# A hybrid decoder trunk: scan states from products of rounded parts, key tiles split a step later, two units multiplied and then added

## The chip, the cores and the metric

The kernel runs on one core of one Trainium2 chip. The metric is the device time of one execution in microseconds (us). The kernel before takes 2855.78 us, the median of three executions (2853.89 to 2859.62).

The names of the engines are those of the profile: PE multiplies matrices (PEld loads its weights), DVE does elementwise work, ACT evaluates functions and copies, POOL does elementwise work too, SP issues DMAs. Each takes its instructions in the order in which the program lists them; between engines they wait for each other.

## The reference, cut to what matters

One sequence of 1024 tokens with 16 learned meta tokens ahead (L = 1040), width 1024, two layers. Layer 0 is a state space mixer (32 heads of 64, in 4 groups that share B and C, state size 128) and a convolutional feed-forward network; layer 1 is a stick-breaking attention (16 heads of 64) and another such network. All inputs and outputs are float32. The part of the mixer that the change touches:

```python
xdt = x_c * dt_c[..., None]
cb = jnp.einsum('bclgn,bcsgn->bgcls', c_c, b_c)
y_diag = jnp.einsum('bgcls,bgecls,bcsgep->bclgep', cb, decay_in, xdt)
decay_to_end = jnp.exp(a_cs[..., -1:] - a_cs)
chunk_states = jnp.einsum('bclgn,bgecl,bclgep->cbgepn', b_c, decay_to_end, xdt)
...
y_off = jnp.einsum('bclgn,cbgepn,bgecl->bclgep', c_c, prev_states, jnp.exp(a_cs))
y = (y_diag + y_off).reshape(b, nc * Q, SSM_D_INNER)[:, pf:pf + L]
```

`chunk_states` is what one chunk of tokens adds to the state; a scan over the chunks scales the state and adds it. The attention multiplies queries by keys, and its output goes through a projection `o @ sb_w_o` that is added to the residual stream `h`.

## The kernel before

**Arithmetic.** Nearly every product of two float32 matrices is made of three products of rounded parts: each operand is split into a high part (a copy rounded to the type fp32r, on ACT) and a low part (the operand minus the high part, on DVE or POOL), and `mm3` (L206) issues high x high, high x low and low x high into one PSUM bank. A few products take float32 operands directly: those of the scan (`cb`, `S`, `y`), transposes and sums.

**The mixer** (`mixer`, L823) scans 4 groups, each over 9 chunks of 116 tokens (the last has 112). The projections of the layer are not done ahead of the scan but between its parts: `work` is a stream of tiles, each one projection of 128 output channels for a third of the tokens (24 products on PE), and the table SHARES says how many tiles go into each chunk: 2 in most chunks of group 0 and group 3, 3 or 4 in groups 1 and 2. A tile ends in a PSUM bank; there are three banks in turn, so a tile needs the bank of the tile three before it. A tile of a convolved projection (all tiles in group 0) is read from its bank by ACT (L336) and three times by DVE (L339), and a SiLU on ACT follows later (L614); a tile of the gate (all in group 3) is read by a SiLU on ACT (L646), then squared on ACT (L658) and worked into sums and products on DVE (L664, L653).

One chunk runs so, in the order of the program:
- `ssd_front` (L759): PE transposes B and x into PSUM and multiplies C by B (`cb`, `px`); ACT copies the transposed B to `bk` (L778); DVE makes `cbm` (L780), `xdt` (L782) and the decayed product `D` (L783); POOL scales `xdt` to `xde`.
- the tiles of `work`. After the first of them the DMAs for the next chunk's `D` and `E` are issued; after the second, DVE subtracts in `D` (L752, 8 instructions) and ACT takes its exponential (L753), for the next chunk.
- `ssd_back` (L789): PE makes the state product `S` from `bk` and `xde` (L799), and DVE adds it to the state (L805); PE makes `y`, 8 products of `xdt` with `D` (L810) and 8 of the state with `E` (L812); DVE adds `y` to x (L814); POOL scales the state for the next chunk.
- POOL scales `E` for the next chunk with C (four pieces), and the next `ssd_front` begins. So POOL's order is: state, `E`, `xde`, and where a weight tile is split in between, its low part `wl`.

Inside the scan the order of PE, DVE, ACT and POOL is that of the program text (a manual schedule); elsewhere, and for SP's queue, a scheduler sets it.

**The attention** runs 8 pairs of heads with 18 steps each. In a step `weigh` multiplies queries by keys into one double bank (`lg`, L1653), ACT takes two sigmoids of it (L1654, L1655), DVE scans and multiplies (L1664, L1665). The projections of the next pair are made in halves between the steps (`half`, L1559). When a key tile is finished, DVE scales it out of its bank (L1577) and returns a function that splits it: `key` (L1583) copies its high part on ACT (L1588), subtracts on DVE (L1589) and issues three DMAs. That function runs in the next step.

**The end of the attention** interleaves the last turns with units of the output projection (`o_blocks`, L1808): a unit is 12 products and one add to `h` on DVE (`accumulate`, L528; the add is L538). Its last part has its own double bank `both`, one half for each of two units.

Of the kernel before, what the change touches and what calls it, by code (L numbers as in the profile page):

```python
# [8 lines left out]
F32 = mybir.dt.float32  # L9
F32R = mybir.dt.float32r  # L10
# [95 lines left out]
class Trunk:  # L106
    def __init__(self, ctx, tc, a):
        self.tc, self.nc, self.a = tc, tc.nc, a
        nc = self.nc
        self.cp = ctx.enter_context(tc.tile_pool(name="cp", bufs=1))  # L110
        self.qp = ctx.enter_context(tc.tile_pool(name="qp", bufs=NQ))
        self.tmps = ctx.enter_context(tc.tile_pool(name="up", bufs=8))
        self.wp = ctx.enter_context(tc.tile_pool(name="wp", bufs=3))
        self.mp = ctx.enter_context(tc.tile_pool(name="mp", bufs=2, space=bass.MemoryType.PSUM))
        self.sp = ctx.enter_context(tc.tile_pool(name="sp", bufs=SMB, space=bass.MemoryType.PSUM))
        self.dp = ctx.enter_context(tc.tile_pool(name="dp", bufs=1, space=bass.MemoryType.DRAM))
        self.lp = None
        self.n = 0
        self.open = []
        self.hold = self.copy_tie = self.silu_tie = None  # L120
        self.consts()


# [404 lines left out]
    def accumulate(self, h, f, s0, n, w, ks, front=0, bank=None, base=0, new=False):  # L528

        ps = (bank or (self.ex if f % 3 == 2 else self.mm))("acc")  # L530
        c, o = slice(s0 - base, s0 - base + n), slice(front + s0, front + s0 + n)
        for i, (hi, lo) in enumerate(ks):
            wh, wl = w(i, f)
            self.mm3(ps[:, :n], wh, wl, hi[:, c], lo[:, c], i == 0, i == len(ks) - 1)
        if new:
            self.nc.vector.tensor_copy(h[f][:, o], ps[:, :n])
        else:
            self.nc.vector.tensor_tensor(h[f][:, o], h[f][:, o], ps[:, :n], op=ALU.add)  # L538

# [219 lines left out]
    def ssd_front(self, g, x, bt, ct, c, dk, pool):  # L759
# [14 lines left out]
        px = px[:n].rearrange("p (h d) -> p h d", h=GH)  # L774
        bk = xde = None
        if c < 8:
            bk = pool.tile([P, P], F32, tag="bk", name=self.nm("bk"), bufs=2)
            nc.scalar.activation(bk[:n], pcb[:n, P : 2 * P], AF.Copy)  # L778
        cbm = pool.tile([P, CB], F32, tag="cbm", name=self.nm("cbm"), bufs=2)
        tt(cbm[:n, :n], pcb[:n, :n], self.past[:n, :n], op=ALU.mult)  # L780
        xdt = pool.tile([P, GH, 64], F32, tag="xdt", name=self.nm("xdt"), bufs=2)
        tt(xdt[:n], px, self.cols[:n, 0, cc, h0 : h0 + GH].unsqueeze(2).to_broadcast([n, GH, 64]), op=ALU.mult)  # L782
        tt(dk, dk, cbm[:n, :n].unsqueeze(1).to_broadcast([n, GH, n]), op=ALU.mult)  # L783
        if c < 8:
            xde = pool.tile([P, GH, 64], F32, tag="xde", name=self.nm("xde"), bufs=2)
            pieces(nc.gpsimd, xde[:n], xdt[:n], self.cols[:n, 2, cc, h0 : h0 + GH].unsqueeze(2).to_broadcast([n, GH, 64]), ALU.mult)
        return xdt, xde, bk

    def ssd_back(self, g, x, c, dk, ce, xdt, xde, bk, states, pool):  # L789

# [3 lines left out]
        cc = 3 * (c % 3) + c // 3  # L794
        e = t0 + n
        state, new = states
        if c < 8:
            ps = self.lg("S")
            nc.tensor.matmul(ps, bk[:n], xde[:n].rearrange("p h d -> p (h d)"), start=True, stop=True)  # L799
            psv = ps.rearrange("p (h d) -> p h d", h=GH)  # L800
            if c == 0:
                new = pool.tile([P, GH, 64], F32, tag="state", name=self.nm("state"), bufs=2)
                nc.scalar.activation(new, psv, AF.Copy)
            else:
                nc.vector.tensor_tensor(new, new, psv, op=ALU.add)  # L805
        py = self.sm("y")
        for i in range(GH):
            q, r = i // 2, 64 * (i % 2)
            y = py[r : r + 64, q * CB : q * CB + n]
            nc.tensor.matmul(y, xdt[:n, i, :], dk[:, i, :], start=True, stop=c == 0)  # L810
            if c:
                nc.tensor.matmul(y, state[:, i, :], ce[:, i, :], start=False, stop=True)  # L812
        for q in range(4):
            nc.vector.scalar_tensor_tensor(x[q][:, t0:e], x[q][:, t0:e], self.par("d_skip", 4 * g + q),  # L814
                                           py[:, q * CB : q * CB + n], op0=ALU.mult, op1=ALU.add)
# [699 lines left out]
    def heads(self, u, p, pool):  # L1515
# [4 lines left out]
        class Pair:  # L1520
# [38 lines left out]
            def half(me, kind, j, h, bank=None, parts=2):  # L1559
# [15 lines left out]
                t = self.tmp(kind)  # L1575
                if kind == "k":
                    nc.vector.tensor_tensor(t[:, :n], ps[:, :n], u[KD][:, o:e], op=ALU.mult)  # L1577
                    return [lambda: me.key(j, t)]
                nc.scalar.activation(t[:, :n], ps[:, :n], AF.Copy)
                me.late.append((j, t))  # L1580
                return []
# [137 lines left out]
    def attention(self, u, pool, hd):  # L1719
# [34 lines left out]
        for kind, j, bank in (("k", 0, self.mm), ("q", 0, self.mm), ("k", 1, self.sm), ("q", 1, self.ex)):  # L1754
            for h in range(2):
                for f in first.half(kind, j, h, bank):
                    f()
            if (kind, j) == ("k", 0):
                self.late_factors()
        self.token_factors(u[KD], pool)  # L1760
        for p in range(PAIRS):
            prev = None
            for n, (i, jj) in enumerate(steps):
# [14 lines left out]
                for own, pair in now.items():  # L1778
                    if p + 1 < PAIRS and (own, n) in halves:
                        late += pair.half(*halves[own, n])  # L1780
                for f in todo + chores[:1]:
                    f()
                del chores[:1]
                for own, pair in now.items():
# [4 lines left out]
        both = self.lg2("acc")  # L1789
        banks = iter([lambda s, a=a: both[:, a] for a in range(2)])  # L1790
        self.unit_bank = lambda s: next(banks, self.mm)(s)
        while turns or ready:
            next(behind)
            next(behind)
            flush(0)
        return od, behind

# [260 lines left out]
```

## Time and profile before

| | us |
|---|---|
| median of three executions | 2855.78 |
| the profiled execution, its own time | 2855.13 |
| its span, first to last instruction | 2853.3 |
| PE busy | 2809.2 |
| DVE busy | 2065.4 |
| ACT busy | 1580.2 |
| POOL busy | 1578.6 |
| scan of the mixer, about | 119 to 614 |
| attention, about | 1545 to 2080 |

The times of the stages are stretches of the span, read from the first and last rows of the stage's lines. In the rows of a timeline the columns are the start, the duration, the engine, the line, the operation, what is written and read with sizes, how many instructions in a row are merged, and in brackets how long the engine sat idle before it and what ended that. A product of float32 operands shows as two instructions. In rows of groups the columns are the count, then busy us and mean ns.

### The profile page before, as it was taken

To read this page: it belongs to the slowest core of one execution; us is meant where nothing else is said; L and a number is where in the kernel's file an instruction comes from. 1 tells how busy PE (TensorE), PEld (TensorE's weight loads), DVE (VectorE), ACT (ScalarE), POOL (GpSimd) and SP (SyncE) were. 2 spreads that over 40 slices of the span, in tenths; PEclk is the share of its full clock that TensorE was granted. 3 is DMA by queue.
4 is the path that set the end of the run, shared out by engine and by line. 5 is a ranking of instruction groups with operands and counts; after the bars stand their busy time and mean duration, and the time that the engine had idled before them with its cause. 6 is when DMAs were issued, how large, how long until landed. Compare 5 with 4: busy or idle time off the path is not lost.

```text
span 2853.3 us, 56464 instructions
## 1 busy us (share of the span) xinstructions
PE 2809.2 (98%) x21251; PEld 2691.9 (94%) x21251; DVE 2065.4 (72%) x3936; ACT 1580.2 (55%) x3077; POOL 1578.6 (55%) x2144
## 2 busy tenths in 40 slices
PE   8999999999999999999999999999999999999998
PEld 7989999999999999999999999999899999999888
DVE  5676666668487676767886888888749676766776
ACT  5554554543256555555335777777536555555433
POOL 2366455553519888867763212112254888886881
PEclk9999999999999999999999999999999999999999
DMA  4333333343413222235142222222532222225331
GB/s 119 86 112 93 121 83 125 116 136 101 120 64 96 78 80 78 79 135 176 49 142 77 74 73 69 80 70 57 184 131 77 82 80 82 75 82 185 111 104 67
DMA packets 141740, 281.78 MB, mean 99 GB/s; under 512 B 16307, under 2 KB 71740, under 8 KB 141468
## 3 DMA queue, kind: packets, MB, share of 16 engines
q1 hardware_dynamic: 135844, 267.01, 29.8%
q0 software_dynamic: 2048, 6.49, 0.6%
q10 hardware_dynamic: 3576, 4.67, 0.5%
q8 instruction: 168, 2.75, 0.4%
q14 instruction: 104, 0.85, 0.1%
HBM read 207.79 MB, written 55.42 MB: 92 GB/s over the span
## 4 chain that ended last, share of the span: by engine, by line
PE 91%; DVE 4%; ACT 2%; POOL 1%; issue 1%; DMA 0%; SPq 0%; ACTq 0%; DVEq 0%; POOLq 0%
PE p L209 10%; PE p L210 10%; PE p L211 10%; PE acc L209 8%; PE acc L211 8%; PE acc L210 8%; PE pj L209 8%; PE pj L210 8%; PE pj L211 8%; PE po L1710 3%; PE lg L1653 2%; PE wT L1687 2%; PE y L810 1%; PE S L799 1%; PE y L812 1%; PE ms L1069 1%
## 5 line engine op out<-in xcount | busy, mean ns | idle before, releaser
L102 POOL TENSOR_TENSOR wl<-w,wh 128x256 fp32r<-128x256 f32 x760 | 678.9, 923 | 352.2 <-ACT wh L196 225.4
L209 PE MATMUL pj<-uh,wh 128*128 128x348 f32 (+2 forms) x1536 | 500.4, 326 | 2.1 <-DVE xbc L339 1.4
L210 PE MATMUL pj<-ul,wh 128*128 128x348 f32 (+2 forms) x1536 | 494.9, 322 | 0.8 <-DVE ul L320 0.8
L211 PE MATMUL pj<-uh,wl 128*128 128x348 f32 (+2 forms) x1536 | 492.0, 320 | 0.0
L209 PE MATMUL p<-bh,fh 128*128 128x262 f32 (+1 forms) x1408 | 400.9, 285 | 3.9 <-DVE p L1237 3.7
L211 PE MATMUL p<-bh,fl 128*128 128x262 f32 (+1 forms) x1408 | 401.0, 285 | 0.9 <-POOL fl L102 0.9
L210 PE MATMUL p<-bl,fh 128*128 128x262 f32 (+1 forms) x1408 | 399.2, 284 | 0.0
L102 POOL TENSOR_TENSOR fl<-x,fh 128x256 fp32r<-128x256 f32 x352 | 264.3, 783 | 186.8 <-ACT fh L1174 160.9
L210 PE MATMUL p<-bl,wh 128*128 128x262 f32 (+1 forms) x1040 | 295.6, 284 | 1.1 <-DVE bl L1098 1.1
L209 PE MATMUL p<-bh,wh 128*128 128x262 f32 (+1 forms) x1040 | 295.3, 284 | 0.4 <-ACT ft L1234 0.4
L211 PE MATMUL p<-bh,wl 128*128 128x262 f32 (+1 forms) x1040 | 294.1, 283 | 0.0
L209 PEld LDWEIGHTS pj<-uh,wh 128*128 128x128 f32 x1536 | 288.7, 188 | 4.5 <-ACT xbc L336 1.7
L210 PEld LDWEIGHTS pj<-ul,wh 128*128 128x128 f32 x1536 | 289.2, 188 | 2.4 <-DVE ul L320 1.4
L211 PEld LDWEIGHTS pj<-uh,wl 128*128 128x128 f32 x1536 | 288.7, 188 | 0.1
L339 DVE SCALAR_TENSOR_TENSOR c<-p,params,c 128x260 f32<-128x260 f32 (+1 forms) x528 | 248.4, 480 | 54.7 <-ACT c L336 48.3
L209 PEld LDWEIGHTS p<-bh,fh 128*128 128x128 f32 x1408 | 268.0, 191 | 4.7 <-DVE p L1237 4.1
L211 PEld LDWEIGHTS p<-bh,fl 128*128 128x128 f32 x1408 | 267.1, 190 | 1.6 <-POOL fl L102 1.5
L210 PEld LDWEIGHTS p<-bl,fh 128*128 128x128 f32 x1408 | 267.8, 190 | 0.5 <-DVE bl L1098 0.4
L1234 ACT ACTIVATE ft<-p 128x262 f32<-128x262 f32 (+1 forms) x352 | 133.2, 382 | 179.9 <-DVE p L1237 110.1
L210 PE MATMUL acc<-gl,wh 128*128 128x260 f32 (+1 forms) x672 | 214.2, 320 | 0.0
L211 PE MATMUL acc<-gh,wl 128*128 128x260 f32 (+1 forms) x672 | 213.2, 319 | 0.0
L209 PE MATMUL acc<-gh,wh 128*128 128x260 f32 (+1 forms) x672 | 210.8, 320 | 0.1
(336 smaller groups left out, 7690.6 us busy)
## 6 DMA issues: line engine op xcount, KB each, us to landing
w<-in_w_up SPq DMA_DIRECT2D x88, 512.0 KB
w<-in_w_down SPq DMA_DIRECT2D x44, 512.0 KB
w<-in_w_in SPq DMA_DIRECT2D x40, 512.0 KB
E<-ea_d SPq DMA_DIRECT2D x32, 464.0 KB
D<-acs_d SPq DMA_DIRECT2D x32, 420.5 KB
g<-c SPq DMA_DIRECT2D x88, 130.0 KB
g<-c SPq DMA_DIRECT2D x88, 128.0 KB
b<-g SPq DMA_DIRECT2D x16, 520.0 KB
```

The source lines that it names most:

```text
L102: done.append(eng.tensor_tensor(out[:, c], x[:, c], y[:, c], op=op))
L209: self.behind(mm(out, wh, uh, start=first, stop=False, skip_group_check=joins), tie, "behind the sums of squares")
L210: mm(out, wh, ul, start=False, stop=False, skip_group_check=joins)
L211: self.last_mm = mm(out, wl, uh, start=False, stop=last, skip_group_check=joins)
L339: ins = nc.vector.scalar_tensor_tensor(out, ps[:, o + i : o + i + n], wcol(i), out, op0=ALU.mult, op1=ALU.add)
L799: nc.tensor.matmul(ps, bk[:n], xde[:n].rearrange("p h d -> p (h d)"), start=True, stop=True)
L810: nc.tensor.matmul(y, xdt[:n, i, :], dk[:, i, :], start=True, stop=c == 0)
L812: nc.tensor.matmul(y, state[:, i, :], ce[:, i, :], start=False, stop=True)
L1234: nc.scalar.activation(s[:, :N], ps[:, :N], AF.Copy)
L1653: nc.tensor.matmul(ps[:nt, a, :m], part[:, c0 : c0 + nt], ks[a][:, s0 : s0 + m], start=x == 0, stop=x == 1)
L1687: nc.tensor.transpose(pt[:ns, x * CB : x * CB + nt], bt[:nt, a, x * CB : x * CB + ns], self.ident[:nt, :nt])
L1710: nc.tensor.matmul(po[64 * a : 64 * a + 64, t0:n], v[: CH[c][1], c, 64 * a : 64 * a + 64], wt[a][q][: CH[c][1], r, t0:n], start=x == 0, st ...
```

## The change

Three edits.

1. **States of the scan.** `bk` becomes two tiles, high (ACT, as before) and low (one more DVE instruction). `xde` is split into `xdh` (ACT) and `xdl` (DVE) by `split_xde`, which `ssd_front` calls right behind POOL's scaling. The state product is an `mm3` of these parts, and it stands behind the 16 products of `y` and not ahead of them. `bk` and `xde` have one buffer each where they had two.
2. **Key tiles.** For the first two thirds of the tokens (j < 2) the function that `half` returns gives back another function, which the loop of the pairs runs a step later; so `key` runs two steps behind the products and not one.
3. **The last two units.** In the first turn of the closing loop the two adds are kept in a list and issued when both units' products have been issued.

```diff
--- before.py
+++ after.py
@@ -117,7 +117,7 @@
         self.lp = None
         self.n = 0
         self.open = []
-        self.hold = self.copy_tie = self.silu_tie = None
+        self.adds = self.hold = self.copy_tie = self.silu_tie = None
         self.consts()
 
 
@@ -534,6 +534,8 @@
             self.mm3(ps[:, :n], wh, wl, hi[:, c], lo[:, c], i == 0, i == len(ks) - 1)
         if new:
             self.nc.vector.tensor_copy(h[f][:, o], ps[:, :n])
+        elif self.adds is not None:
+            self.adds.append(lambda: self.nc.vector.tensor_tensor(h[f][:, o], h[f][:, o], ps[:, :n], op=ALU.add))
         else:
             self.nc.vector.tensor_tensor(h[f][:, o], h[f][:, o], ps[:, :n], op=ALU.add)
 
@@ -774,17 +776,25 @@
         px = px[:n].rearrange("p (h d) -> p h d", h=GH)
         bk = xde = None
         if c < 8:
-            bk = pool.tile([P, P], F32, tag="bk", name=self.nm("bk"), bufs=2)
-            nc.scalar.activation(bk[:n], pcb[:n, P : 2 * P], AF.Copy)
+            bk = pool.tile([P, 2, P], F32R, tag="bk", name=self.nm("bk"), bufs=1)
+            nc.scalar.activation(bk[:n, 0], pcb[:n, P : 2 * P], AF.Copy)
+            tt(bk[:n, 1], pcb[:n, P : 2 * P], bk[:n, 0].bitcast(F32), op=ALU.subtract)
         cbm = pool.tile([P, CB], F32, tag="cbm", name=self.nm("cbm"), bufs=2)
         tt(cbm[:n, :n], pcb[:n, :n], self.past[:n, :n], op=ALU.mult)
         xdt = pool.tile([P, GH, 64], F32, tag="xdt", name=self.nm("xdt"), bufs=2)
         tt(xdt[:n], px, self.cols[:n, 0, cc, h0 : h0 + GH].unsqueeze(2).to_broadcast([n, GH, 64]), op=ALU.mult)
         tt(dk, dk, cbm[:n, :n].unsqueeze(1).to_broadcast([n, GH, n]), op=ALU.mult)
         if c < 8:
-            xde = pool.tile([P, GH, 64], F32, tag="xde", name=self.nm("xde"), bufs=2)
-            pieces(nc.gpsimd, xde[:n], xdt[:n], self.cols[:n, 2, cc, h0 : h0 + GH].unsqueeze(2).to_broadcast([n, GH, 64]), ALU.mult)
+            xde = [pool.tile([P, GH, 64], dt, tag=t, name=self.nm(t), bufs=1) for t, dt in (("xdh", F32R), ("xdl", F32R), ("xde", F32))]
+            pieces(nc.gpsimd, xde[2][:n], xdt[:n], self.cols[:n, 2, cc, h0 : h0 + GH].unsqueeze(2).to_broadcast([n, GH, 64]), ALU.mult)
+            self.split_xde(xde, c)
         return xdt, xde, bk
+
+    def split_xde(self, xde, c):
+
+        hi, lo, t = (t[: CH[c][1]] for t in xde)
+        self.nc.scalar.activation(hi, t, AF.Copy)
+        self.nc.vector.tensor_tensor(lo, t, hi.bitcast(F32), op=ALU.subtract)
 
     def ssd_back(self, g, x, c, dk, ce, xdt, xde, bk, states, pool):
 
@@ -794,15 +804,6 @@
         cc = 3 * (c % 3) + c // 3
         e = t0 + n
         state, new = states
-        if c < 8:
-            ps = self.lg("S")
-            nc.tensor.matmul(ps, bk[:n], xde[:n].rearrange("p h d -> p (h d)"), start=True, stop=True)
-            psv = ps.rearrange("p (h d) -> p h d", h=GH)
-            if c == 0:
-                new = pool.tile([P, GH, 64], F32, tag="state", name=self.nm("state"), bufs=2)
-                nc.scalar.activation(new, psv, AF.Copy)
-            else:
-                nc.vector.tensor_tensor(new, new, psv, op=ALU.add)
         py = self.sm("y")
         for i in range(GH):
             q, r = i // 2, 64 * (i % 2)
@@ -810,6 +811,16 @@
             nc.tensor.matmul(y, xdt[:n, i, :], dk[:, i, :], start=True, stop=c == 0)
             if c:
                 nc.tensor.matmul(y, state[:, i, :], ce[:, i, :], start=False, stop=True)
+        if c < 8:
+            ps = self.lg("S")
+            hi, lo = (t[:n].rearrange("p h d -> p (h d)") for t in xde[:2])
+            self.mm3(ps, bk[:n, 0], bk[:n, 1], hi, lo, True, True)
+            psv = ps.rearrange("p (h d) -> p h d", h=GH)
+            if c == 0:
+                new = pool.tile([P, GH, 64], F32, tag="state", name=self.nm("state"), bufs=2)
+                nc.scalar.activation(new, psv, AF.Copy)
+            else:
+                nc.vector.tensor_tensor(new, new, psv, op=ALU.add)
         for q in range(4):
             nc.vector.scalar_tensor_tensor(x[q][:, t0:e], x[q][:, t0:e], self.par("d_skip", 4 * g + q),
                                            py[:, q * CB : q * CB + n], op0=ALU.mult, op1=ALU.add)
@@ -1575,7 +1586,7 @@
                 t = self.tmp(kind)
                 if kind == "k":
                     nc.vector.tensor_tensor(t[:, :n], ps[:, :n], u[KD][:, o:e], op=ALU.mult)
-                    return [lambda: me.key(j, t)]
+                    return [lambda: [lambda: me.key(j, t)] if j < 2 else me.key(j, t)]
                 nc.scalar.activation(t[:, :n], ps[:, :n], AF.Copy)
                 me.late.append((j, t))
                 return []
@@ -1754,7 +1765,8 @@
         for kind, j, bank in (("k", 0, self.mm), ("q", 0, self.mm), ("k", 1, self.sm), ("q", 1, self.ex)):
             for h in range(2):
                 for f in first.half(kind, j, h, bank):
-                    f()
+                    for g in f() or ():
+                        g()
             if (kind, j) == ("k", 0):
                 self.late_factors()
         self.token_factors(u[KD], pool)
@@ -1778,7 +1790,9 @@
                 for own, pair in now.items():
                     if p + 1 < PAIRS and (own, n) in halves:
                         late += pair.half(*halves[own, n])
-                for f in todo + chores[:1]:
+                for f in todo:
+                    late += f() or []
+                for f in chores[:1]:
                     f()
                 del chores[:1]
                 for own, pair in now.items():
@@ -1789,9 +1803,13 @@
         both = self.lg2("acc")
         banks = iter([lambda s, a=a: both[:, a] for a in range(2)])
         self.unit_bank = lambda s: next(banks, self.mm)(s)
+        self.adds = []
         while turns or ready:
             next(behind)
             next(behind)
+            for f in self.adds or ():
+                f()
+            self.adds = None
             flush(0)
         return od, behind
```

**How the instructions move.** The first place is ACT in one chunk of group 0 (`bk` is the transposed B, `pj` a projection tile in its bank, `D` the decays). Before:

```order
L778 ACTIVATE bk_1598<-cb_1590 116x128
L336 ACTIVATE xbc_1519<-pj_1608,params 128x348
L614 ACT_TABLE_LOAD
L614 ACTIVATE xbc_1519<-xbc_1519 128x348
L336 ACTIVATE xbc_1519<-pj_1642,params 128x344
L614 ACTIVATE xbc_1519<-xbc_1519 128x348
L753 ACT_TABLE_LOAD
L753 ACTIVATE D_1638<-D_1638 116x928
L778 ACTIVATE bk_1720<-cb_1712 116x128
```

The same chunk after the change:

```order
L780 ACTIVATE bk_1619<-cb_1611 116x128
L796 ACTIVATE xdh_1627<-xde_1629 116x512
L336 ACTIVATE xbc_1538<-pj_1634,params 128x348
L616 ACT_TABLE_LOAD
L616 ACTIVATE xbc_1538<-xbc_1538 128x348
L336 ACTIVATE xbc_1538<-pj_1668,params 128x344
L616 ACTIVATE xbc_1538<-xbc_1538 128x348
L755 ACT_TABLE_LOAD
L755 ACTIVATE D_1664<-D_1664 116x928
L780 ACTIVATE bk_1748<-cb_1740 116x128
```

The copy of `xde`, which POOL writes, now stands ahead of both tiles of the chunk in ACT's queue.

The second place is ACT in a pair of the attention (`kp` and `bt` are the sigmoids, `wt` transposed weights, `k` the key tile's copy). Before:

```order
L1654 ACTIVATE kp_18955<-lg_18958,rt_18460 116x2x348
L1655 ACTIVATE bt_18956<-lg_18958,rt_18459 116x2x348
L1588 ACTIVATE k_18684<-k_18932 128x348
L1554 ACTIVATE wh_18987<-w_2404_18942,params 128x128 x4
L1693 ACTIVATE wt_18801<-wT_18997 116x3x116
L1693 ACTIVATE wt_18803<-wT_19002 116x3x116
L1654 ACTIVATE kp_19007<-lg_19010,rt_18460 116x2x348
L1655 ACTIVATE bt_19008<-lg_19010,rt_18459 116x2x348
```

The same steps after the change:

```order
L1665 ACTIVATE kp_19179<-lg_19182,rt_18684 116x2x348
L1666 ACTIVATE bt_19180<-lg_19182,rt_18683 116x2x348
L1565 ACTIVATE wh_19205<-w_2468_19166,params 128x128 x4
L1704 ACTIVATE wt_19025<-wT_19215 116x3x116
L1704 ACTIVATE wt_19027<-wT_19220 116x3x116
L1665 ACTIVATE kp_19225<-lg_19228,rt_18684 116x2x348
L1666 ACTIVATE bt_19226<-lg_19228,rt_18683 116x2x348
L1599 ACTIVATE k_18908<-k_19156 128x348
```

The key tile's copy stands one pair of sigmoids later; DVE's subtraction moves with it.

The third place is PE at the end of the attention, where the second of the two units begins (the rows name the semaphores on which an instruction waits). Before:

```order
L209 MATMUL acc_25466<-o_24904,wh_25222 128x256
L210 MATMUL acc_25466<-o_24904,wh_25222 128x256
L211 MATMUL acc_25466<-o_24904,wl_25223 128x256
L209 MATMUL acc_25466<-o_25069,wh_25222 128x256 [waits DVE_49]
L210 MATMUL acc_25466<-o_25069,wh_25222 128x256
L211 MATMUL acc_25466<-o_25069,wl_25223 128x256
```

After the change:

```order
L209 MATMUL acc_25690<-o_25128,wh_25446 128x256
L210 MATMUL acc_25690<-o_25128,wh_25446 128x256
L211 MATMUL acc_25690<-o_25128,wl_25447 128x256
L209 MATMUL acc_25690<-o_25293,wh_25446 128x256
L210 MATMUL acc_25690<-o_25293,wh_25446 128x256
L211 MATMUL acc_25690<-o_25293,wl_25447 128x256
```

The products stand where they stood; the second unit's wait for DVE (for the add of the first unit, which reads the other half of the same tile) is gone.

## The prediction

> **What bounds the kernel now.** I read the page first: the span, the engines' shares, and the chain of work that ended last.
>
> ```profile
> span 2853.3 us, 56464 instructions
> PE 2809.2 (98%) x21251; PEld 2691.9 (94%) x21251; DVE 2065.4 (72%) x3936; ACT 1580.2 (55%) x3077; POOL 1578.6 (55%) x2144
> PE 91%; DVE 4%; ACT 2%; POOL 1%; issue 1%; DMA 0%; SPq 0%; ACTq 0%; DVEq 0%; POOLq 0%
> ```
>
> PE is busy for 98% of the span and holds 91% of the chain, so every microsecond of PE counts, and every wait of PE is paid in full. Next, what PE waits for; of the rows these four stand where the change works:
>
> ```profile
> PE lg L1653 <- ACT bt L1655: 6.3, 11, 0.8
> PE acc L209 <- DVE h L538: 4.3, 2, 3.3
> PE y L810 <- DVE D L783: 1.5, 1, 1.5
> PE S L799 <- POOL xde L102: 1.4, 3, 0.6
> ```
>
> Eleven waits on a sigmoid, two on an add, and hardly any in the scan. But the shares are means. The third view is the chain in order of time, for the cadence of the chunks with two tiles (group 0, then group 3):
>
> ```profile
> 146.31 0.86 PE S L799 x2
> 191.36 0.86 PE S L799 x2
> ...
> 551.03 1.13 PE S L799 x2
> 597.53 0.86 PE S L799 x2
> ```
>
> Four chunks each: 11.26 us and 11.6 us a chunk. The fourth is the timeline of one chunk of group 0, engine by engine (POOL, then ACT, DVE, PE):
>
> ```profile
> 155.71 1.18 POOL L102 TENSOR_TENSOR xde<-xdt,cols 116x256 f32<-116x256 f32 x2
> 162.34 1.19 POOL L102 TENSOR_TENSOR state<-state,cd 128x256 f32<-128x256 f32 x2 [5.46 <-DVE state L805]
> 163.49 3.50 POOL L102 TENSOR_TENSOR E<-E,xbc 128x232 f32<-128x232 f32 x4
> 166.96 1.18 POOL L102 TENSOR_TENSOR xde<-xdt,cols 116x256 f32<-116x256 f32 x2
> ...
> 153.78 0.64 ACT L336 ACTIVATE xbc<-pj,params 128x348 f32<-128x348 f32 x1 [2.24 <-PE pj L211]
> 154.44 1.28 ACT L614 ACT_TABLE_LOAD   x1
> 155.73 0.50 ACT L614 ACTIVATE xbc<-xbc 128x348 f32<-128x348 f32 x1
> 157.62 0.64 ACT L336 ACTIVATE xbc<-pj,params 128x344 f32<-128x344 f32 x1 [1.39 <-PE pj L211]
> 162.68 1.05 ACT L196 ACTIVATE wh<-w 128x1024 fp32r<-128x1024 f32 x1
> ...
> 158.29 1.80 DVE L339 SCALAR_TENSOR_TENSOR xbc<-pj,params,xbc 128x344 f32<-128x344 f32 x3 [2.02 <-ACT xbc L336]
> 160.00 1.60 DVE L752 TENSOR_SCALAR D<-D,cols 116x116 f32<-116x116 f32 x8
> 161.51 0.68 DVE L805 TENSOR_TENSOR state<-state,S 128x512 f32<-128x512 f32 x1
> ...
> 157.42 1.02 PE L799 MATMUL S<-xde,bk 116*128 116x512 f32 x2
> ```
>
> The reader is to see how late POOL is: `xde` ends at 156.89, half a microsecond before PE takes it at 157.42. POOL sat idle for 5.46 us ahead of its state, but what it does stands in a row: second tile on ACT, DVE's three passes, the decay subtraction, the state's add, then POOL's state, `E`, `xde`. That row is 10.5 us long (from 157.62 to 168.14, the end of the next `xde`) against a cadence of 11.26. It doesn't bind, by 0.5 us.
>
> **The change part by part.** *The state product.* Its price before is 0.86 us on the chain. The new one is three products 512 wide; products of that width and kind run 0.24 us apart in the network at the end:
>
> ```profile
> 2689.87 0.40 PE L211 MATMUL acc<-gh,wl 128*128 128x512 f32 x1
> 2690.11 0.40 PE L209 MATMUL acc<-gh,wh 128*128 128x512 f32 x1
> ```
>
> 3 x 0.23 = 0.69, so 0.2 us less for each of 32, 6.4 us in all, wherever PE sets the pace.
>
> *The split.* The copy `xdh` is new; nearest is a copy of the same width on ACT, and for `xdl` DVE's add to the state, of the same width (0.68 at 161.51 above):
>
> ```profile
> L803 ACT ACTIVATE state<-S x4: 580/592/596, 128.3 to 521.7; 128x512 f32<-128x512 f32 x4
> ```
>
> So 0.59 and about 0.68 us, and for `bk`'s low part, a quarter as wide, an estimate of 0.3. As work that is little. As a wait it is not: `xdh` waits for POOL, and ACT has both tiles of the chunk behind it. In the chunk shown it could start at 168.14, while the first tile's copy ran at 165.02 before. And now the row closes into a ring: `xde`, `xdh`, first tile, SiLU, second tile, DVE, state, `E`, `xde`. From start to start, by the rows above:
>
> xdh 0.59; first tile 0.66 (153.78 to 154.44); table 1.29; SiLU 0.50; second tile until DVE 0.67 (157.62 to 158.29); convolution 1.71 (to 160.00); decay 1.51 (to 161.51); state's add until POOL 0.83 (to 162.34); POOL's state 1.15; `E` 3.47; `xde` 1.18. Sum 13.6 us.
>
> Where a weight tile is split, 1.05 us more (L196, one tile in three, so two chunks in three): 14.3 in the mean, against 11.1 that PE needs now (11.26 less 0.2). Between the first and the last but one chunk of group 0 lie seven passes: 7 x (14.3 - 11.26) = 21 us. In the last chunk `y` waits for `D` already now (1.5 us above), and `D` comes behind the same hops; I add 1. **Group 0: +22.** Nothing covers this: PE has products for three tiles ahead at most, and `y` stands between.
>
> Group 3 has the same ring with shorter tiles:
>
> ```profile
> 546.94 0.46 ACT L646 ACTIVATE z<-pj 128x348 f32<-128x348 f32 x1 [0.57 <-PE pj L211]
> 547.30 0.49 ACT L658 ACTIVATE z<-xbc 128x348 f32<-128x348 f32 x1
> 551.98 0.51 DVE L653 TENSOR_TENSOR xbc<-xbc,z 128x344 f32<-128x344 f32 x1
> 552.41 1.60 DVE L752 TENSOR_SCALAR D<-D,cols 116x116 f32<-116x116 f32 x8
> ```
>
> xdh 0.59, table 1.29, two tiles with their squares 1.6 (0.36 + 0.40 + 0.36 + 0.48), sum and product on DVE 0.87, decay 1.52, then 0.83 + 1.15 + 3.47 + 1.18 as above: 12.5, and 13.2 with the weight copy in two chunks of three. Against 11.6: 1.6 a chunk over six chunks, 9.6, less about 1 that the first chunks have in hand. **Group 3: +9.**
>
> Groups 1 and 2 have 3 or 4 tiles a chunk and room:
>
> ```profile
> 414.00 1.74 POOL L102 TENSOR_TENSOR xde<-xdt,cols 116x256 f32<-116x256 f32 x2
> 423.62 1.02 PE L799 MATMUL S<-xde,bk 116*128 116x512 f32 x2
> ```
>
> `xde` is ready 8 us ahead. Sixteen state products save 3 us. Against it, in a chunk of four tiles the fourth needs the first one's bank, which ACT empties only behind `xdh`: I put 0 to 4 us a group, take 1.5, so **groups 1 and 2: 0** together (-3 to +5).
>
> *Key tiles.* In each of seven pairs ACT sits idle for the key tile's product, and PE then waits for the sigmoids behind it:
>
> ```profile
> 1577.24 0.50 ACT L1588 ACTIVATE k<-k 128x348 fp32r<-128x348 f32 x1 [1.20 <-DVE k L1577]
> 1581.11 0.68 PE L1653 MATMUL lg<-k,qs 128*116 128x232 f32 x4 [0.65 <-ACT bt L1655]
> ```
>
> A step later the product is long there. 7 x 0.65 = **-4.5** (bounds 0, if another sigmoid is late, and -6.3, all the waits of this kind). The key tiles' DMAs go out one step later on SP: the first tile's at step 11 of 18, read at the next pair's first step, the second's at the last step, read at the next pair's fourth. Nobody waits for them.
>
> *The two units.* The second unit waits for the first one's add, which stands behind scans on DVE, and PE's clock falls behind that wait:
>
> ```profile
> 2061.03 0.58 PE L209 MATMUL acc<-o,wh 128*128 128x256 f32 x1 [3.31 <-DVE h L538]
> 2061.00:2064.00 3.00, 2.97 (x14) 2.75 (x16) 0.01 (x1) 0.00 (x0) 0.00 (x0) 0.50 0.99 371
> 2064.00:2067.00 3.00, 3.00 (x20) 2.01 (x22) 0.42 (x1) 0.00 (x0) 0.00 (x0) 0.52 1.01 373
> ```
>
> The wait of 3.31 goes, and the 6 us at half clock (0.50 and 0.52) that cost 3: **-6.3** (bounds -3.3, if the clock falls for another reason, and -6.3). What stands behind on PE is the values' product, whose weights ACT wrote ahead of the second unit, so I let nothing be late next.
>
> Sum: 22 + 9 + 0 - 4.5 - 6.3 = +20, on the profiled execution's 2855.1 (0.7 under the median): **2875 us**. The ends of the unknown lie on POOL:
>
> ```profile
> L102 POOL TENSOR_TENSOR E<-E,xbc x128: 654/686/1590, 130.1 to 599.6; 128x232 f32<-128x232 f32 x112, 128x224 f32<-128x224 f32 x16
> ```
>
> Four pieces at their shortest are 2.6 us and not 3.5, 0.9 less a pass; upwards `xde` took 1.74 in group 1, 0.6 more. On 13 passes that is -11 and +7.
>
> **The clock.** The wait of 3.31 us was followed by half clock; the one of 1.5 in front of `y`, in this stretch, was not (the third number from the end is the clock):
>
> ```profile
> 209.00:213.00 4.00, 2.53 (x37) 2.24 (x37) 3.93 (x9) 2.96 (x4) 0.00 (x0) 1.00 0.34 102
> ```
>
> The ring makes waits of 2 to 3 us a chunk and a longer one in front of the last `y` of group 0; where between 1.5 and 3.3 the limit lies no row shows. [...]
>
> **The rivals.** *The ring doesn't bind* (12%). ACT stands, but POOL's row would have to end 2.5 us earlier each chunk; then PE sets the pace everywhere: -6.4 - 4.5 - 6.3 = -17, 2838 us. For it: before the change the scan shows 1.4 us of waits for POOL, and ACT is busy only 55%. Against it: the ring's 13.6 is made of rows of this stage, without a wait in it but one semaphore's hop each. It decides at a ring of 11.1.
>
> *The ring is shorter than counted* (10%). POOL's pieces at their shortest (13.6 - 0.9 = 12.7) and the weight copy beside a wait: 1.5 x 7 + 2 in group 0, nothing in group 3, -3 in groups 1 and 2, -10.8 behind: about -1, 2854 us, no change. For it: DVE will be idle more, and POOL's pieces spread with what DVE does. Against it: DVE's own row (`cbm`, `xdt`, `D`) runs beside `E` as before.
>
> *The clock falls in every chunk of groups 0 and 3* (12%). It decides if waits of 2 to 3 us are enough. A fall costs 3 us, as above; in group 0 the ring hides it (11.1 + 3 is under 14.3), in group 3 it is 0.9 a chunk too much (14.1 against 13.2), 5 us, and 3 at the last `y`: +28, 2883 us.
>
> *The change doesn't do what it says*: the order shows that it does, so no chance is kept for that.
>
> **How the numbers follow.** The forecast, 2875, has 66%; its own range by the ends above is 2862 to 2888. No change means within 0.2% (5.7 us, 2850 to 2861.5), about what a measurement of this kernel can tell. Faster: the first rival and a bit of the second, 14%; same: most of the second, 7%; slower: the rest, 79%. The range leaves out the first rival and little else: 2848 to 2893.
>
> **What would show it.** PE's waits in the scan: `y` for `E` or `D` and `S` for `xdl`, some 2.5 us a chunk in group 0 and under 2.5 in group 3, where now 2.9 stand in all; ACT idle in front of `xdh` for POOL, 2 to 6 us each time; the cadence of `S` in group 0 at 13.6 to 14.6. In the attention no wait of 0.65 for the sigmoids in the first seven pairs, and full clock at 2061 less the shift. It is wrong if the cadence of group 0 stays under 12.

## The result, and the profile after

The changed kernel takes 2893.52 us, the median of four executions (2892.71 to 2894.45), beside 2855.55 for the kernel before in the same runs: ratio 1.0129, 95% interval 1.0115 to 1.0143. It is slower by 38 us, where the forecast was 20. As a time it lies half a microsecond above the end of the range (2893); as a ratio to the kernel before it lies just inside (1.0129 x 2855.78 = 2892.6).

The page after (its span, the engines' busy time, the chain by engine):

```profile
span 2892.2 us, 56651 instructions
PE 2822.5 (98%) x21283; PEld 2708.5 (94%) x21283; DVE 2101.1 (73%) x4000; ACT 1597.5 (55%) x3109; POOL 1576.7 (55%) x2144
PE 76%; DVE 11%; ACT 5%; POOL 4%; issue 3%; DMA 1%; DVEq 0%; ACTq 0%; SPq 0%; POOLq 0%
```

Busy shares say almost nothing: ACT and POOL stand at 55% as before. The chain says it: PE's part falls from 91% to 76%, and DVE, ACT and POOL take its place. The waits after (engine, line, releaser: us in all, times, the longest), those that grew or went:

```profile
PE y L811 <- DVE D L786: 12.7, 7, 5.0
PE S L209 <- ACT xdh L796: 10.6, 11, 1.2
PE pj L209 <- DVE xbc L339: 6.3, 3, 2.5
PE ms L676 <- DVE xbc L825: 3.0, 1, 3.0
PE lg L1664 <- ACT bt L1666: 1.8, 4, 0.8
ACT xdh L796 <- POOL xde L102: 169.5, 32, 6.9
```

The last row is the cause's trace: ACT stands 169.5 us in front of `xdh`, at all 32 chunks, until POOL has `xde`. (Of the three waits in front of `pj`, one, of 1.4 us, stands ahead of the scan and was there before.) Seven of the eleven sigmoid waits in the attention are gone, and so is the 3.31 us in front of the second unit.

The chain in order of time shows one whole turn of the ring in group 0 (start, duration, what):

```profile
195.08 0.63 ACT xdh L796
195.71 0.53 ACT xbc L336
196.26 1.28 ACT L616
197.55 0.50 ACT xbc L616
198.20 0.70 issue
198.90 0.63 ACT xbc L336
...
201.37 1.94 DVE D L754 x8
203.31 0.60 DVE state L823
204.05 1.19 POOL state L102 x2
205.24 0.69 POOL E L102 x2
...
208.71 1.15 POOL xde L102 x2
209.89 0.63 ACT xdh L796
```

From `xdh` to `xdh` 14.81 us, and PE is not in it. (The 0.70 of "issue" is ACT at the weight copy; the second half of `E` is left out in front of `xde`.) Where each group's first product `cb` starts, after less before, gives the account. The starts are those of the timeline's `cb` rows; c8 is a group's last chunk:

| | g0 c1 | g0 c8 | g1 c0 | g2 c0 | g3 c0 | g3 c8 | whole span |
|---|---|---|---|---|---|---|---|
| after less before, us | +0.2 | +20.1 | +25.0 | +30.6 | +34.7 | +49.6 | +38.9 |

The columns give +20 over the chunks of group 0, +5 at its last `y`, +9.7 in groups 1 and 2, +14.9 in group 3, and -10.7 behind the scan.

### The profile page after: what moved, and what is told of

Same layout as the page of the kernel before. It is cut to its first block, busy times and chain, and to the rows that moved or that the text cites. A ratio compares the mean times of both kernels' runs of the same rounds, so it can differ in the third digit from the quotient of the medians.

```text
span 2892.2 us, 56651 instructions
## 1 busy us (share of the span) xinstructions
PE 2822.5 (98%) x21283; PEld 2708.5 (94%) x21283; DVE 2101.1 (73%) x4000; ACT 1597.5 (55%) x3109; POOL 1576.7 (55%) x2144
## 4 chain that ended last, share of the span: by engine, by line
PE 76%; DVE 11%; ACT 5%; POOL 4%; issue 3%; DMA 1%; DVEq 0%; ACTq 0%; SPq 0%; POOLq 0%
PE p L211 10%; PE p L210 10%; PE p L209 10%; PE acc L209 8%; PE acc L210 8%; PE acc L211 8%; PE pj L209 4%; PE pj L210 4%; PE pj L211 4%; DVE D L754 2%; DVE kp L1675 2%; PE po L1721 2%; PE lg L1664 2%; PE wT L1698 2%; POOL E L102 1%
```

## The experiments

Unless a diff says otherwise, each is a small edit of the changed kernel. Ratios are to the kernel before in the same runs (2854.2 to 2854.8 us). The theory: ACT, held in its queue in front of `xdh`, closes the ring. The rivals: the added work itself, DVE's wait for `xdl`, the order of `y` and `S`, the attention edits. The cadence of group 0 is the distance of its `cb` rows, from c1 or c2 to c8.

### The scan edit undone, the attention edits kept

```diff
-            bk = pool.tile([P, 2, P], F32R, ...)      # xdh, xdl, split_xde, mm3 and the order of y and S likewise
+            bk = pool.tile([P, P], F32, tag="bk", ...)
+            nc.tensor.matmul(ps, bk[:n], xde[:n].rearrange("p h d -> p (h d)"), start=True, stop=True)
```

> The scan layer's edit is undone (one float32 product for the states, ahead of y, no parts); the key tiles' and the two units' edits stay. Theory (the scan edit alone is the loss, the attention edits are worth what stands between the end of the scan and the end of the kernel): of the +38.9 us of the profiled span, +49.6 stood at the end of the scan and -10.7 came behind it, so this should be 10.7 under the kernel before: 2845 us, the chunks of group 0 at their 11.3 us cadence again. Rival (the 10.7 us are not the attention edits' own but slack that a later scan gives to what is loaded or computed behind it): 2855, no change from the kernel before.

Measured 2844.34 us, ratio 0.9958 (0.9941 to 0.9974), the starts of all 36 chunks 0.8 before those of the kernel before, group 0's cadence 11.2 to 11.3 from c2 on (from c1 to c2 it is 12.1 in both). The scan edit alone is the loss, 49 us of it; the other two edits are a gain of 10.4. This kernel beats both.

### Each attention edit alone, on the kernel before

```diff
-                    return [lambda: me.key(j, t)]
+                    return [lambda: [lambda: me.key(j, t)] if j < 2 else me.key(j, t)]
```

> The kernel before with the key tiles' edit alone (split one group later). Forecast's term: -4.5, 2850.5 beside the kernel before in the same runs (ratio 0.9984). Rival (the two attention edits do the same work twice over, or the units' edit alone carries the 10.5 us between the kernel before and the one with the scan undone): 2854 or 2844.

Measured 2849.86, ratio 0.9986 (0.9977 to 0.9995): 4.3 less. PE's waits in the attention, with the key tiles' edit alone:

```profile
PE acc L209 <- DVE h L540: 4.3, 2, 3.3
PE lg L1655 <- ACT bt L1657: 1.8, 4, 0.8
```

The other one is the three places that collect and issue the adds:

```diff
+        elif self.adds is not None:
+            self.adds.append(lambda: self.nc.vector.tensor_tensor(h[f][:, o], h[f][:, o], ps[:, :n], op=ALU.add))
```

> The kernel before with the two units' edit alone (last two units multiplied, then added). Forecast's term: -6.3, 2848.7 (ratio 0.9978). With both edits together measured at 10.4 under the kernel before, the two single runs should add up to 10 to 11 if the terms are independent; rival: 2854 or 2844, one edit carrying all of it.

Measured 2848.84, ratio 0.9980 (0.9972 to 0.9989): 5.3 less. Its waits are the mirror image, and the clock at this place (third number from the end) stays whole:

```profile
PE lg L1655 <- ACT bt L1657: 6.3, 11, 0.8
PE acc L209 <- DVE h L540: 1.0, 1, 1.0
...
2059.00:2062.00 3.00, 3.00 (x32) 2.24 (x27) 1.46 (x5) 0.92 (x4) 0.00 (x0) 1.00 0.86 289
2062.00:2065.00 3.00, 3.00 (x29) 3.00 (x27) 0.80 (x2) 0.45 (x3) 0.00 (x0) 1.00 0.98 329
```

4.3 + 5.3 = 9.6 beside 10.4 for both: the two terms are independent, as far as runs that differ by some us among themselves can tell.

### The wait for POOL taken away, the work left

```diff
-            self.split_xde(xde, c)
+            self.split_xde(xde[:2] + [xdt], c)
```

> The changed kernel with one other operand: xdh and xdl stand where they stood but are made from xdt, which DVE has written before, and no longer from POOL's xde, which is still computed and read by nobody. So the decay to the chunk's end is left out of the state products; all instructions, their sizes and their order are the same. It takes the wait for POOL away and nothing else. Theory (that wait closes the ring): group 0's cadence 11.1 to 11.5 us in place of 14.2, 2838 to 2850. Rival A (the added work or its place ahead of the tile costs, not the wait): within 5 us of 2893; half and half would be 2865 to 2870.

Measured 2840.04, ratio 0.9945 (0.9930 to 0.9960). Same instructions, same sizes, same places in the queues, 53 us less. Group 0's cadence is 11.1 to 11.2 from c2 on, the bank waits of groups 1 and 2 are gone, and of PE's waits in the scan two of more than 1 us are left, one of 1.3 in front of `ms` and this one:

```profile
PE y L811 <- DVE D L786: 2.2, 1, 2.2
```

That settles wait against work. ACT still sits idle in front of `xdh` here, 69.8 us in all, but for DVE's `xdt`, which comes early: its idle time in itself cost nothing here. The single buffers of the change stand here too, so they are not what costs the 53 us. Against the run with the scan undone this one is 4.3 us faster. The chunks of three tiles in groups 1 and 2 take 0.11 us less each (14.72 against 14.83), which over 32 chunks would be 3.5; by the profiles the last chunk starts only 2.9 earlier, and where the rest comes from is not shown.

### Both parts made behind the first tile

```diff
-            self.split_xde(xde, c)                     # in ssd_front
+                                if c < 8:              # in the loop of the chunk, behind its first tile
+                                    self.split_xde(ops[1], c)
```

> The changed kernel with one move: both parts of xde (xdh on ACT, xdl on DVE) are issued behind the chunk's first weight tile and no longer ahead of it; the instructions and their number are the same. Theory (ACT stands in its queue in front of xdh until POOL has xde, and with it the tile's table and SiLU, DVE's decay, POOL's state and E: a ring of 13.6 to 14.3 us against 11.1 us that PE needs): the ring opens, group 0's cadence falls from 14.2 to 11.1-11.5, groups 0 and 3 give back some 25 and 12 of their 25 and 15 us; the bank wait of groups 1 and 2 (2.5 us and what follows it, 9.7 in both) may stay: 2838 to 2850. Rival A (the ring is not the wait but the work that was added to ACT, DVE and PE): within 5 us of 2893. Rival B (S on PE now waits for xdl, since it is made a tile later): each of the 28 chunks that waits pays 1 us or more, 2865 or above.

Measured 2853.70, ratio 0.9997 (0.9987 to 1.0007): 40 us better than the change and no better than the kernel before. Both rivals are out, but the expectation's number did not hold: group 0's cadence was 11.2 to 12.6, mean 11.9. That fits a ring that got shorter by the first tile's copy, table and SiLU but did not open (POOL, then ACT, then DVE):

```profile
157.68 1.19 POOL L102 TENSOR_TENSOR xde<-xdt,cols 116x256 f32<-116x256 f32 x2
168.88 1.18 POOL L102 TENSOR_TENSOR xde<-xdt,cols 116x256 f32<-116x256 f32 x2
180.62 1.17 POOL L102 TENSOR_TENSOR xde<-xdt,cols 116x256 f32<-116x256 f32 x2
...
158.90 0.63 ACT L795 ACTIVATE xdh<-xde 116x512 fp32r<-116x512 f32 x1 [3.09 <-POOL xde L102]
159.43 0.62 ACT L336 ACTIVATE xbc<-pj,params 128x344 f32<-128x344 f32 x1
...
170.75 1.23 DVE L796 TENSOR_TENSOR xdl<-xde,xdh 116x512 fp32r<-116x512 f32 x1 [1.96 <-ACT xdh L795]
```

ACT still waits 3.09 us for POOL, and the second tile stands behind `xdh`. From the first `xde` to the second lie 11.20 us, the length of PE's work, and to the third 11.74; there `xdl` took 1.23 us on DVE, where its median in the changed kernel is 0.69. The row of 10.5 us that the prediction measured before the change needs only `xdh`'s 0.6 to fill the cadence.

### Only the low part moved

```diff
-            self.split_xde(xde, c)
+            nc.scalar.activation(xde[0][:n], xde[2][:n], AF.Copy)
...
+                                if c < 8:              # behind the first tile: the low part on DVE
...
+                                    self.nc.vector.tensor_tensor(lo, t, hi.bitcast(F32), op=ALU.subtract)
```

> The changed kernel with only DVE's part moved: xdl (DVE) is issued behind the chunk's first weight tile, xdh (ACT) stays ahead of it and waits for POOL as before. Theory (it is ACT's wait that closes the ring; DVE's xdl lies beside it, with 1.2 to 1.3 us from xdh's start to xdl's end and the tile's product on DVE not due until ACT's table and SiLU are done): 2893, give or take 6, group 0's cadence still 13.5 to 14.5. Rival C (DVE's wait in front of xdl holds the second tile's product, conv and decay and closes the ring as well): group 0's cadence falls to 12.5 or less, 2875 or under.

Measured 2904.55, ratio 1.0172 (1.0156 to 1.0187). DVE's wait does not close the ring: with it out of the way ACT still waits 170.2 us in front of `xdh` and group 0 still runs at 13.1 to 15.7. That it got 11 us worse than the change, 5 beyond the expectation, was not foreseen:

```profile
PE S L210 <- DVE xdl L897: 30.1, 15, 3.7
```

PE now stands between the first and second product of `S`, because `xdl` comes behind a convolution on DVE, and with it stand the next chunk's products. Its clock falls oftener, too: at ten places in the scan, where 18.8 us are lost by slices of 1 us, against six places and 12 us with the change.

### `E` behind `xde` on POOL

```diff
-                        for _ in ahead:                # E of this chunk, ahead of ssd_front
-                            pass
...                                                    # (a count that keeps the decay ahead of ssd_front)
                         ops = self.ssd_front(g, x, bt, ct, c, dk, pool)
+                        for _ in ahead:
+                            pass
```

> The changed kernel with one exchange on POOL: the chunk's E product is issued behind xde and no longer ahead of it; xdh and xdl stand ahead of the tile and wait for POOL's xde as before. It leaves the wait in place and takes E's 3.5 us out of what the wait contains. Theory (the length of the ring decides, and E is a term of it): 14.2 - 3.5 = 10.7 us, under the 11.1 to 11.2 that PE needs, so group 0's cadence goes to 11.2-11.7 and the time to 2838 to 2852. Rival (any wait of ACT for POOL ahead of the tile costs its 1 to 3 us a chunk, whatever stands ahead of xde on POOL): cadence 12.5 or more, 2870 or above. Rival on the other side (the chunk's E comes too late for y): PE waits for E in front of the second products of y, which it does not do in the changed kernel.

Measured 2872.28, ratio 1.0061 (1.0047 to 1.0075). Group 0's cadence is 11.5 to 14.1, mean 12.6 from c1 to c8. By these numbers the theory failed: both lie where the first rival put them (12.5 or more, 2870 or above). 1.6 of 14.2 us are gone with `E`, not its 3.5. Two rows on PE and POOL lead to the reason:

```profile
PE y L813 <- POOL E L102: 8.3, 14, 1.3
POOL xde L102 <- DVE xdt L785: 60.0, 24, 14.6
```

`y` now waits for `E`, the rival on the other side. And POOL now waits for DVE's `xdt` 24 times (11 with the change): a second branch was hidden behind `E`. It runs along DVE's own queue, from the decay over the adds to the state and of `y` to x, `bk`'s low part and `cbm` to `xdt`, and from there to `xde` (POOL, then DVE):

```profile
182.19 1.93 POOL L102 TENSOR_TENSOR xde<-xdt,cols 116x256 f32<-116x256 f32 x2 [0.78 <-DVE xdt L785]
195.07 1.94 POOL L102 TENSOR_TENSOR xde<-xdt,cols 116x256 f32<-116x256 f32 x2 [0.78 <-DVE xdt L785]
...
190.35 2.01 DVE L754 TENSOR_SCALAR D<-D,cols 116x116 f32<-116x116 f32 x8
...
192.88 1.06 DVE L825 SCALAR_TENSOR_TENSOR xbc<-xbc,params,y 128x116 f32<-128x116 f32 x4
...
194.25 0.67 DVE L785 TENSOR_TENSOR xdt<-px,cols 116x512 f32<-116x512 f32 x1
```

From `xde` to `xde` 12.88 us, with a weight copy in it, and again a closed row of work without PE. So what was taken out of one branch counted only down to the next: the rows fit a ring whose length decides. The rival, a price for each of ACT's waits whatever stands ahead of `xde`, is not ruled out by this run's numbers; the waits are still there, 144.4 us in all.

### `xde` on DVE

```diff
+            tt(xde[2][:n], xdt[:n], self.cols[:n, 2, cc, h0 : h0 + GH]..., op=ALU.mult)    # ahead of D
         tt(dk, dk, cbm[:n, :n].unsqueeze(1).to_broadcast([n, GH, n]), op=ALU.mult)
-            pieces(nc.gpsimd, xde[2][:n], xdt[:n], ..., ALU.mult)
```

> The changed kernel with xde computed by DVE, right behind xdt, in place of POOL; xdh and xdl stand where they stood. All the parts and products of the change are kept, and the output is the same. Theory (the wait for POOL is what costs; one more product of some 0.7 us on DVE fits under PE): near the run whose parts were made from xdt, 2840 to 2848, group 0's cadence 11.1 to 11.6. Rival (DVE, which paces what comes before D, becomes the bound with one more product a chunk): group 0's cadence 12 or more, 2855 or above. This would be faster than the kernel with the scan edit undone (2844.3) only where the states' products, smaller on PE than the float32 one, are worth something.

Measured 2848.33, ratio 0.9976 (0.9967 to 0.9985), 0.3 us above the end of the expectation. All of the change's arithmetic is there, 45 us under the change. Group 0's cadence is 11.2 to 12.0 from c2 on, 0.4 above what was expected at most; groups 1 to 3 lose nothing. What it still pays stands at the last `y` of group 0, and in the clock behind it (0.50 from 216 to 218 us):

```profile
PE y L812 <- DVE D L789: 6.7, 7, 3.3
```

### The order of `y` and `S` alone, on the kernel before

```diff
+        py = self.sm("y")                              # and y's products, ahead of S
         if c < 8:
             ps = self.lg("S")
             nc.tensor.matmul(ps, bk[:n], xde[:n].rearrange("p h d -> p (h d)"), start=True, stop=True)
```

> The kernel before with one exchange: y's products are issued ahead of the one float32 states product. Theory (the order of the two is not what costs, the wait for POOL is): within 2 us of the kernel before, 2853 to 2856, group 0's cadence 11.2 to 11.3. Rival (the states' product behind y sends state to DVE and POOL later, and so part of the changed kernel's loss): 2860 or above.

Measured 2856.73, ratio 1.0008 (0.9999 to 1.0017), group 0's cadence 11.28 to 11.33: 2.2 us more in the same runs, where at most 2 were expected, and not to be told from zero by the interval. In the profile a chunk of three tiles in groups 1 and 2 takes 14.89 us, where the kernel before takes 14.83. So the order is not what the changed kernel lost.

### Group 0 with the float32 product, the rest with `xde` on DVE

```diff
+            if g:                                      # rounded parts in groups 1 to 3
+                self.split_xde(xde, c)
+            else:                                      # float32 product in group 0
+                pieces(nc.gpsimd, xde[0][:n], xdt[:n], dec, ALU.mult)
```

> The attention edits, the states in rounded parts with xde on DVE in groups 1 to 3, and in group 0, where chunks carry two tiles and the ring has the least room, the float32 product with xde on POOL as in the kernel before. Theory: group 0 as in the kernel before (no loss of 5 us, of which 3.3 us at the last y, that the run with xde on DVE everywhere had there), 0.1 us a chunk gained in groups 1 and 2, next to nothing in group 3: 1.8 to 2 us under the run with the scan edit undone (2844.3), so 2841.5 to 2843.5. Rival (rounded parts gain nothing that can be seen): 2844 to 2846; 2850 or above if group 3 is held by DVE.

In group 0 `y` still stands ahead of `S`. Measured 2842.12, ratio 0.9961 (0.9949 to 0.9974). By the median that is within the expectation. But its five executions lie between 2840.8 and 2847.9, and the interval covers the ratio of the run with the scan undone (0.9958). Nor was group 0 without loss: in the profiled execution, the longest of the five, its last chunk took 1.7 us more than in the kernel before. The chunks show the 0.1 us gained each in groups 1 and 2; that this version is the better one is not shown.

## Why the prediction was right, and where not

**The time: inside the range partly by luck.** It lies at the end of the stated range and 5 us beyond the forecast's own one (2862 to 2888). The wider range was drawn for the rivals, the highest of them a clock that falls in every chunk, and that did not happen. What filled it were three terms that all came out too small: the last `y`, groups 1 and 2, and group 3. The mechanism is what was right.

**The ring and its length: right.** The forecast counted 13.6 us and 14.3 in the mean from rows of before; the chunks c1 to c8 of group 0 came 13.3 to 14.9 apart, mean 14.2, and the seven passes cost 20 where 21 were predicted. Term by term, the head of one turn on ACT after:

```profile
180.69 0.63 ACT L796 ACTIVATE xdh<-xde 116x512 fp32r<-116x512 f32 x1 [5.43 <-POOL xde L102]
181.23 1.04 ACT L196 ACTIVATE wh<-w 128x1024 fp32r<-128x1024 f32 x1
182.18 0.63 ACT L336 ACTIVATE xbc<-pj,params 128x348 f32<-128x348 f32 x1
182.82 1.28 ACT L616 ACT_TABLE_LOAD   x1
```

From start to start: `xdh` 0.54, weight copy 0.95, first tile 0.64, table 1.30, where 0.59, 1.05, 0.66 and 1.29 stood in the sum. From `xdh` to `xdh` a turn without a weight copy took 13.4 us, with one 14.4 or 14.8; counted were 13.6 and 14.6. That the wait and not the work makes it is shown by the run whose parts came from `xdt`; that its length decides rests on these turns and on the rows of the run with `E` taken out. The sign on PE was right in kind, but `S` waits for `xdh` (10.6 us), not for `xdl`.

**The last `y` of group 0: right in kind, too small.** The term was "I add 1". The wait grew by 3.5 and the clock fell behind it (wait in brackets, then the clock):

```profile
234.93 0.75 PE L811 MATMUL y<-D,xdt 112*64 112x112 f32 x4 [4.98 <-DVE D L786]
...
234.93:240.93 6.00, 6.00 (x44) 5.72 (x45) 4.17 (x15) 1.21 (x1) 0.00 (x0) 0.52 0.24 37
```

Together +5 at the next group's start and 1 more in its first chunk. The prediction had a fall of the clock behind this wait, at 3 us, in a rival alone and not in its main sum; 3.4 were lost. And the forecast treated this chunk like the others, but it has one tile, so PE arrives there a tile earlier, while `D` comes at the ring's end: the lag of the ring behind PE falls due at once.

**Groups 1 and 2: the largest miss.** The prediction named the right mechanism (the fourth tile needs the first one's bank, which ACT empties only behind `xdh`), put 0 to 4 us on it a group, took 1.5, and set 3 us of smaller products against it: 0. Measured +9.7. Once a group PE waits 2.5 us and the clock falls for 3.4 us behind it:

```profile
352.98 0.40 PE L209 MATMUL pj<-uh,wh 128*128 128x348 f32 x1 [2.46 <-DVE xbc L339]
503.49 0.56 PE L209 MATMUL pj<-uh,wh 128*128 128x348 f32 x1 [2.45 <-DVE xbc L339]
...
352.98:357.00 4.02, 4.02 (x16) 4.02 (x17) 3.95 (x7) 1.67 (x2) 4.02 (x7) 0.58 0.20 51
503.49:507.49 4.00, 4.00 (x15) 4.00 (x16) 3.93 (x7) 1.67 (x2) 4.00 (x7) 0.57 0.16 53
```

2.46 + 4.02 x 0.42 = 4.1, which is what this chunk lost in each of the two groups. Group 1's c0 and c3 and group 2's c3 lost another 1.1, 0.9 and 0.6, the first of them to the clock left low by group 0. The gain was over-rated, too: 0.2 us a chunk was put, 0.11 came (14.83 to 14.72). The prediction's own rows had the products 0.24 apart and the sum took 0.23; and with the order of `y` and `S` already changed the products save 0.17 (14.89 to 14.72), of which the order takes back 0.06, a term that the sum did not have.

**Group 3: a hop was missed.** 12.5 us were counted, 13.5 with a weight copy and 13.2 in the mean; measured were 13.46 (from the `xde` at 589.52 to that at 602.98) and, with a copy, 14.95; five turns in a row had 14.4 in the mean. The second square on ACT reads a product of DVE (L655) that stands behind the sum of the first square, so the path runs ACT, DVE, ACT, DVE, where in the count ACT's four instructions ran on without a wait:

```profile
593.42 0.45 ACT L648 ACTIVATE z<-pj 128x344 f32<-128x344 f32 x1
594.60 0.50 ACT L660 ACTIVATE z<-xbc 128x348 f32<-128x348 f32 x1 [0.73 <-DVE xbc L655]
```

The wait is 0.73 us here and 1.27 in the next turn. The rows of before had been laid end to end without asking of each what it reads. One more loss was not in the count: in c6 PE waits 2.95 us for the sum `ms`, and the clock falls behind it (0.50 from 630 to 633 us). In all +14.9 in place of +9.

**The attention: right.** -10.7 behind the scan against -10.8; alone, 4.3 against 4.5 and 5.3 against 6.3.

**The clock.** Its rival wanted a fall in every chunk. It fell at six places in the scan after, and in most chunks not. But the main sum had nothing for it, and that was wrong as well: by slices of 1 us (one less the granted clock, added up from 116 to 668) 12 us were lost, 1.7 at each place and twice that behind the last `y`; before lost none. How much of the fall inside group 0's ring was hidden by the ring no run tells.

Sum of the misses, measured less predicted: group 0 -0.9 and +4 (ring and last `y`), groups 1 and 2 +9.7, group 3 +5.9, behind 0.1: 18.8, against 18.5 between 2893.5 and 2875. What the clock lost is contained in these terms.

## What to carry to other kernels

Before an instruction is put at the head of an in-order queue, follow from what it waits for back to what stands behind it: if that path returns, the loop's length competes with the bounding engine, as 14.2 us a turn did here with PE's 11.1 to 11.2, while ACT and POOL were busy for 55% of the span. A ring can be measured ahead of time from the rows before (14.3 counted here), but look for what it meets when it becomes late: here the short stage at its end (+5 us), the buffer that is freed behind it (+9.7), and the next longest branch, which left 1.6 us a chunk of the 3.5 that went with `E`. Here the copy made one tile later gave back 40 us, its operand made on an engine with room 45, of the 53 that the wait cost.

## What the runs showed of the hardware

**The clock fell behind waits of 2.46, 2.45 and 1.91 us, and not behind others of 2.43 to 2.66.** The two bank waits of 2.46 and 2.45 us above were followed by half clock (0.50 from 354 to 356 us and from 504 to 506). With `E` behind `xde` the same two waits were not:

```profile
338.62 0.40 PE L209 MATMUL pj<-uh,wh 128*128 128x348 f32 x1 [2.43 <-DVE xbc L339]
488.87 0.40 PE L209 MATMUL pj<-uh,wh 128*128 128x348 f32 x1 [2.44 <-DVE xbc L339]
...
338.62:342.62 4.00, 4.00 (x24) 3.79 (x24) 3.93 (x7) 1.67 (x2) 4.00 (x7) 1.00 0.16 53
488.87:492.87 4.00, 4.00 (x24) 3.79 (x24) 3.93 (x7) 1.66 (x2) 4.00 (x7) 1.00 0.18 54
```

In the run with group 0 in float32 a lone wait of 1.91 us was followed by it as well (0.50 from 212 to 215 us); in the run with the low part moved, waits of 2.55 and 2.66 were not. Each fall in the scan lost 1.7 us, which is 3.4 us at half clock, or twice that: behind the wait of 5 us, and once behind one of 2.48 in the run with the low part moved. So the length of a wait did not settle in these runs whether the clock fell; what else decides is not shown.

**Beside `D` on DVE, `xde` on POOL took 1.93 to 2.08 us, and 1.18 alone.** In the changed kernel 17 of the 32 `xde` ran while DVE stood idle and took 1.18 or 1.19 us (so did the one at 168.88 above); the other 15 ran while DVE's `D` did and took 1.93 to 2.08. In the turn at 195 us with `E` behind `xde` it was 1.94:

```profile
194.85 1.11 DVE L786 TENSOR_TENSOR D<-D,cbm 116x928 f32<-116x928 f32 x1
```

`D` ends at 195.96, `xde` at 197.01, 1.05 us later, a little less than its own 1.18. Not every neighbour did this to POOL: in the kernel before, `E` took 3.50 us beside `xdt`, `D` and a convolution (163.49 to 166.99), but 2.61 beside the decay (223.38 to 225.99), and there the decay took 3.90, where at 160.00, with POOL idle, it took 1.60. The 1.23 us of `xdl` above, where 0.69 is its median in the changed kernel, began while POOL was at a weight's low part (170.02 to 173.26). Why the one or the other takes longer is not shown. A step that is moved is to be priced beside its new neighbour.
